# One late load piece of a streaming dot-product kernel, split over partitions as 120 + 8

## The chip, the cores and the metric

The kernel runs on one core of a Trainium2 chip. The metric is device time in microseconds (us); lower is better. Runs agree within about 0.3% (the kernel before took 323.23 to 324.14 us in nine runs of one series). The profiled executions have a span about 2 us shorter than the device time (321.6 against 323.7 us before the change); spans are compared only with spans.

Words used below: SyncE issues the loads, VectorE multiplies and sums, and the DMA engines, 16 by the profile's count, move the data. A *packet* is one entry of the trace's DMA records, with its size and the time it took. In the loads of 128 partitions it is the part of one partition (14 loads each of x and y at 32 KB a partition left 3584 packets of 32 KB). A *landing count* is one of the semaphore increments that a load leaves in the trace; a load of 128 partitions leaves 16. A count is read here as the share of one engine having arrived, and a load as landed when all its counts have come.

## The reference

```python
B, N, D = 8, 4096, 512                      # x, y: float32
gram = np.matmul(x, y.transpose(0, 2, 1))
diag = np.diagonal(gram, axis1=1, axis2=2)  # only x[b,n] . y[b,n] is needed
diag = diag - diag.max(axis=-1, keepdims=True)
exp = np.exp(diag)
return exp / exp.sum(axis=-1, keepdims=True)
```

Only the 8 x 4096 row products matter: 134 MB are read, and almost nothing is written.

## The kernel before

Each batch is laid out as 32 rows of 2 KB per partition and loaded in two halves of 16 rows. The very last half comes in pieces of 8, 4, 2, 1 and 1 rows, so that little work is left once the last bytes land. x and y of a piece are two loads, all issued by SyncE. The loads share eight semaphores, so a load also waits for the landing of the one eight before it (the last y is issued at 305.97 us, 0.02 us after y of the 8-row piece has landed).

```python
H = R // 2                                   # 16 rows
xv = x.rearrange("b (p r) d -> b p r d", p=P)   # partition p: rows 32p .. 32p+31
...
def load(b, r0, parts):
    xt = io.tile([P, H, D], f32, tag="xt", name="xt")      # io has 3 buffers
    yt = io.tile([P, H, D], f32, tag="yt", name="yt")
    o = 0
    for n in parts:
        nc.sync.dma_start(out=xt[:, o : o + n, :], in_=xv[b, :, r0 + o : r0 + o + n, :])
        nc.sync.dma_start(out=yt[:, o : o + n, :], in_=yv[b, :, r0 + o : r0 + o + n, :])
        o += n
    return xt, yt
...
def dots_by_row(b, r0, xt, yt):              # one VectorE operation a row
    for k in range(H):
        c = b * R + r0 + k
        nc.vector.scalar_tensor_tensor(out=xt[:, k, :], in0=xt[:, k, :], scalar=1.0,
            in1=yt[:, k, :], op0=mult, op1=mult, accum_out=diag[:, c : c + 1])
...
n = 2 * b + h
parts = {2 * B - 2: [8, 8], 2 * B - 1: [8, 4, 2, 1, 1]}.get(n, [H])
```

## Time and profile before

| | kernel before |
|---|---|
| time, median of the first 3 runs | 323.7 us (323.36 to 323.76) |
| profiled span | 321.6 us |
| DMA over the span | 418 GB/s |
| VectorE busy | 261.4 us (81%) |

From the page of the kernel before: the span; DMA's busy share (in tenths) and GB/s in 40 equal slices; and the chain that ended last, by engine.

```profile
span 321.6 us, 345 instructions
...
DMA  8999999999999999999999999999999999999991
GB/s 326 456 395 452 440 408 456 391 458 391 456 412 436 454 395 456 440 408 458 416 432 456 392 458 440 408 456 417 433 449 395 456 437 412 424 424 426 427 407 53
...
DMA 63%; DVE 33%; issue 1%; SPq 1%; POOL 1%; ACT 0%; POOLq 0%; DVEq 0%
```

The DMA engines are busy from the first slice to the last but one (tenths of 8 and 9): the kernel is bound by its load stream. The chain in order of time (start us, us, what) shows its end.

```profile
275.00 30.96 DMA yt<-in_y_dram
305.95 0.02 issue
305.97 10.16 DMA yt<-in_y_dram
316.13 0.02 issue
316.15 0.71 DVE xt L58 x2
```

The very last load, y of the last row, lands at 316.13 us. Some 5.5 us of softmax and store follow. VectorE's timeline (start us, us, engine, line, operation, and in brackets the idle time before it and what ended it) shows the last three pieces, of 2, 1 and 1 rows:

```profile
313.60 0.69 DVE L58 SCALAR_TENSOR_TENSOR xt<-xt,yt 128x512 f32<-128x512 f32 x1
314.22 0.08 DVE L58 DVE_READ_ACCUMULATOR xt<-xt,yt 128x1 f32 x1
314.22 0.69 DVE L58 SCALAR_TENSOR_TENSOR xt<-xt,yt 128x512 f32<-128x512 f32 x1
314.83 0.08 DVE L58 DVE_READ_ACCUMULATOR xt<-xt,yt 128x1 f32 x1
314.95 0.69 DVE L58 SCALAR_TENSOR_TENSOR xt<-xt,yt 128x512 f32<-128x512 f32 x1
315.57 0.08 DVE L58 DVE_READ_ACCUMULATOR xt<-xt,yt 128x1 f32 x1
316.15 0.69 DVE L58 SCALAR_TENSOR_TENSOR xt<-xt,yt 128x512 f32<-128x512 f32 x1 [0.50 <-DMA yt<-in_y_dram]
```

Of these rows VectorE waits only before the very last, for 0.50 us.

Now the window view: stretch, its length, busy us and operations of VectorE, ScalarE and GpSimd, the clock, the DMA busy share and GB/s.

```profile
306.00:310.00 4.00, 4.00 (x13) 0.00 (x0) 0.00 (x0) 1.00 0.99 412
310.00:312.00 2.00, 1.94 (x7) 0.00 (x0) 0.00 (x0) 1.00 1.01 402
312.00:314.00 2.00, 1.97 (x7) 0.00 (x0) 0.00 (x0) 1.00 1.05 389
314.00:316.00 2.00, 1.61 (x6) 0.00 (x0) 0.00 (x0) 1.00 0.36 130
```

The loads go at about 400 GB/s up to 314 us (412, 402, 389), then taper (130 GB/s, a DMA busy share of 0.36). The landing counts are read from the trace's semaphore records (first, fifteenth and sixteenth count in us):

```
kernel before                first   15th    16th
y of the 8-row piece        304.77  305.11  305.95
y of the 4-row piece        309.75  310.10  310.94
y of the 2-row piece        312.32  312.65  313.50
y of the last row but one   313.68  314.01  314.86
y of the last row           315.01  315.32  316.13
```

Fifteen counts come within 0.35 us, and one is 0.8 us late, every time: read as engines, one is late. Before 240 us no load shows such a count (the sixteenth count comes at most 0.12 us after the fifteenth). At 241.08 us the instruction queue (q14) fetched 8192 B in 0.333 us; a 32 KB packet that began as it ended took 1.875 us, where 1.213 us is usual (the median of 3584).

### The profile page before, as it was taken

The page shows a single profiled execution, that of the slowest core. Times are in us where ns is not written, and L with a number is a line of the kernel's source. Part 1 is how long each engine was busy: PE and PEld are TensorE (multiplying, and loading weights), DVE is VectorE, ACT ScalarE, POOL GpSimd, SP SyncE. Part 2 cuts the span into 40 slices and gives each one's busy share as a digit, 9 for nine tenths or more (in the row PEclk, how much of TensorE's full clock was granted, in tenths as well). Part 3 has the DMA queues.
Part 4 walks back from the last instruction along what each step waited for, and adds up shares of the span by engine and source line. Part 5 has one row for each costly group of instructions (what it writes and reads, how often), then busy time and mean ns, then how long its engine had stood idle before and what let it go on. Part 6 is the DMA issues. An engine that isn't in the chain of part 4 may idle for free.

```text
span 321.6 us, 345 instructions
## 1 busy us (share of the span) xinstructions
DVE 261.4 (81%) x154; ACT 4.6 (1%) x17; POOL 6.1 (2%) x20
## 2 busy tenths in 40 slices
DVE  0019979898998979979799897989979799776494
ACT  1000000000000000000000000000000000000000
POOL 0000000000000000000000000000000000000000
DMA  8999999999999999999999999999999999999991
GB/s 326 456 395 452 440 408 456 391 458 391 456 412 436 454 395 456 440 408 458 416 432 456 392 458 440 408 456 417 433 449 395 456 437 412 424 424 426 427 407 53
DMA packets 7201, 134.36 MB, mean 418 GB/s; under 512 B 1824, under 2 KB 1824, under 8 KB 2592
## 3 DMA queue, kind: packets, MB, share of 16 engines
q1 hardware_dynamic: 6048, 134.22, 97.5%
q10 hardware_dynamic: 1152, 0.13, 0.3%
q14 instruction: 1, 0.01, 0.0%
HBM read 134.22 MB, written 0.13 MB: 418 GB/s over the span
## 4 chain that ended last, share of the span: by engine, by line
DMA 63%; DVE 33%; issue 1%; SPq 1%; POOL 1%; ACT 0%; POOLq 0%; DVEq 0%
DMA yt<-in_y_dram 63%; DVE xt L50 16%; DVE diag L51 16%; SPq L43 1%; POOL mx L74 0%; POOL ssum L83 0%; DVE mxp L72 0%; DVE xt L58 0%; ACT res L78 0%; DVE rc L85 0%; POOLq L121 0%; SPq L44 0%; DVE res L86 0%; DVE nmx L76 0%; DVEq L50 0%
## 5 line engine op out<-in xcount | busy, mean ns | idle before, releaser
L50 DVE TENSOR_TENSOR xt<-xt,yt 128x8192 f32<-128x8192 f32 x13 | 113.0, 8689 | 34.5 <-DMA yt<-in_y_dram 34.5
L51 DVE TENSOR_REDUCE diag<-xt 128x16 f32<-128x8192 f32 x13 | 112.9, 8686 | 0.4
L58 DVE SCALAR_TENSOR_TENSOR xt<-xt,yt 128x512 f32<-128x512 f32 x48 | 30.0, 687 | 9.9 <-DMA yt<-in_y_dram 9.7
L74 POOL PARTITION_ALL_REDUCE mx<-mxp x8 | 2.8, 352 | 306.6 <-DVE mxp L72 306.6
L85 DVE RECIPROCAL rc<-ssum 128x1 f32<-128x1 f32 x8 | 1.3, 164 | 7.7 <-POOL ssum L83 7.7
L78 ACT ACTIVATE res<-diag,nmx 128x32 f32<-128x32 f32 x8 | 2.6, 321 | 312.9 <-DVE nmx L76 312.9
L76 DVE TENSOR_SCALAR nmx<-mx 128x1 f32<-128x1 f32 x8 | 1.2, 154 | 4.3 <-POOL mx L74 4.3
L58 DVE DVE_READ_ACCUMULATOR xt<-xt,yt 128x1 f32 x48 | 3.9, 82 | 0.0
L83 POOL PARTITION_ALL_REDUCE ssum<-sump x8 | 3.1, 385 | 5.8 <-ACT res L78 5.8
L86 DVE TENSOR_SCALAR res<-res,rc 128x32 f32<-128x32 f32 x8 | 1.9, 242 | 0.9
L72 DVE TENSOR_REDUCE mxp<-diag 128x1 f32<-128x32 f32 x8 | 1.5, 186 | 0.3
L78 ACT ACTIVATION_READ_ACCUMULATOR res<-diag,nmx 128x1 f32 x8 | 1.5, 186 | 0.0
L78 ACT ACT_TABLE_LOAD x1 | 1.3, 1283 | 0.7 <-PEq L110 0.7
L110 POOL MEMSET const-float32-0.0<- 128x1 f32 x1 | 0.1, 100 | 0.2 <-issue 0.2
L110 POOL MEMSET const-bfloat16-1.0<- 128x1 bf16 x1 | 0.1, 102 | 0.0
L110 POOL MEMSET const-uint8-127<- 128x1 uint8 x1 | 0.1, 102 | 0.0
L110 POOL MEMSET const-float32-1.0<- 128x1 f32 x1 | 0.1, 99 | 0.0
## 6 DMA issues: line engine op xcount, KB each, us to landing
xt<-in_x_dram SPq DMA_DIRECT2D x14, 4096.0 KB, 31.2
yt<-in_y_dram SPq DMA_DIRECT2D x14, 4096.0 KB, 40.5
xt<-in_x_dram SPq DMA_DIRECT2D x3, 2048.0 KB, 27.1
yt<-in_y_dram SPq DMA_DIRECT2D x3, 2048.0 KB, 31.6
xt<-in_x_dram SPq DMA_DIRECT2D x1, 1024.0 KB, 31.9
yt<-in_y_dram SPq DMA_DIRECT2D x1, 1024.0 KB, 29.5
xt<-in_x_dram SPq DMA_DIRECT2D x1, 512.0 KB, 25.8
yt<-in_y_dram SPq DMA_DIRECT2D x1, 512.0 KB, 22.2
```

The lines of the kernel that those rows point to most:

```text
L43: nc.sync.dma_start(out=xt[:, o : o + n, :], in_=xv[b, :, r0 + o : r0 + o + n, :])
L50: nc.vector.tensor_tensor(out=xt, in0=xt, in1=yt, op=mybir.AluOpType.mult)
L51: nc.vector.tensor_reduce(out=diag[:, c : c + H], in_=xt, axis=mybir.AxisListType.X, op=mybir.AluOpType.add)
L58: nc.vector.scalar_tensor_tensor(out=xt[:, k, :], in0=xt[:, k, :], scalar=1.0, in1=yt[:, k, :], op0=mybir.AluOpType.mult, op1=mybir.AluOpT ...
L72: nc.vector.tensor_reduce(out=mxp, in_=db, axis=mybir.AxisListType.X, op=mybir.AluOpType.max)
L74: nc.gpsimd.partition_all_reduce(out_ap=mx, in_ap=mxp, channels=P, reduce_op=bass_isa.ReduceOp.max)
L76: nc.vector.tensor_single_scalar(out=nmx, in_=mx, scalar=-1.0, op=mybir.AluOpType.mult)
L78: nc.scalar.activation(out=rb, in_=db, func=mybir.ActivationFunctionType.Exp, bias=nmx, scale=1.0, accum_out=sump,)
L83: nc.gpsimd.partition_all_reduce(out_ap=ssum, in_ap=sump, channels=P, reduce_op=bass_isa.ReduceOp.add)
L85: nc.vector.reciprocal(out=rc, in_=ssum)
L86: nc.vector.tensor_single_scalar(out=rb, in_=rb, scalar=rc, op=mybir.AluOpType.mult)
L110: nc = _bacc.Bacc("TRN2", target_bir_lowering=False, num_devices=1)
```

## The change

The piece that holds the last row but one is cut over the partitions, into 120 and 8. By its stated purpose these go over 15 and over 8 DMA engines. So one gets nothing of the larger part. A likely intent is to let a late engine catch up by the end.

```diff
         for n in parts:
-            nc.sync.dma_start(out=xt[:, o : o + n, :], in_=xv[b, :, r0 + o : r0 + o + n, :])
-            nc.sync.dma_start(out=yt[:, o : o + n, :], in_=yv[b, :, r0 + o : r0 + o + n, :])
+            cut = 120 if n == 1 and o == H - 2 else P
+            for p0, p1 in ((0, cut), (cut, P)):
+                if p0 < p1:
+                    nc.sync.dma_start(out=xt[p0:p1, o : o + n, :], in_=xv[b, p0:p1, r0 + o : r0 + o + n, :])
+                    nc.sync.dma_start(out=yt[p0:p1, o : o + n, :], in_=yv[b, p0:p1, r0 + o : r0 + o + n, :])
             o += n
```

## The prediction

> **What bounds the kernel.** The loads. Slices of the page: DMA 90% or more in almost every slice, 418 GB/s over 321.6 us. The chain of waits ends: DMA y 275.00 to 316.13, last row's multiply 316.15, then softmax and store. So only the end of the load stream matters; the 5.5 us after it are fixed.

> **Who is late at the end.** Each load leaves 16 landing counts in the trace[...]. Fifteen come within 0.38 us and the sixteenth 0.8 to 0.86 us after them, in nearly every load since 246 us (before: 0.05 to 0.12 us). The last y piece: fifteen from 315.01 to 315.32, the last at 316.13. The lag was born at 241.08 us, where the instruction queue (q14) fetched 8192 B in 0.333 us and the next 32 KB packet took 1.875 us instead of 1.213. It was never worked off[...].

> **What the change does.** [...] Then one engine gets none of the last piece but one. 16 packets of 2 KB at 84 to 86 ns, about 1.36 us, leave it[...]. If the skipped engine is the late one (not shown; I give it 85%), it becomes early by about 0.5 us[...].

> **How much is on the critical path.** Not all 0.65 us. In the timeline VectorE runs back to back from 305.98 (y of the 8-row piece landed): 15 rows at 0.61 us and four hand-overs, ending the last row but one at 315.57, so that the last row can't start before about 315.69. It started at 316.15 (0.50 us idle before it): the gain is at most 0.46 us.

> **Costs.** Two more SyncE issues (0.33 to 0.43 us each), off the path: loads share eight semaphores, so each waits for the one eight back. The last y now waits for y of the 4-row piece (landed 310.94) instead of the 8-row piece (305.95), when about 4 us of work are queued: no hole. The last row but one waits on four semaphores instead of two, some 0.02 to 0.06 us.

> **The risk.** [...] This would eat the gain or turn it to a loss of up to 1 us.

> **Time.** Without conflict 323.7 - 0.46 = 323.25; with weights for the failures, 323.35 us; 8 in 10: 322.8 to 324.1. Faster by over 2%: 0.01; within 2%: 0.98; slower: 0.01.

> **What would show it.** The last y: no straggler, all counts within some 0.5 us, the end at about 315.5 to 315.7; VectorE's 0.50 us idle before the last row falls to about 0. Everything before 313.5 us unchanged, the lag of 0.84 us still there for the 2-row piece. Wrong: the straggler still at 0.8 us (it isn't the skipped engine), or 2 KB packets well over 90 ns[...], or a hole before the last packets (late issue).

The last y was to land at about 315.5 us instead of 316.13, some 0.65 us earlier: the fifteenth count at 315.32, and 0.17 us for two more packets of 86 ns on eight engines. VectorE allowed 0.46 us of this gain: 323.7 - 0.46 = 323.25 us. The risk was slower packets, at most 1.4 us for this piece (an estimate that lets each of an engine's 16 packets of 86 ns take as long again; that they would was not shown). Weights for the failures added 0.1 us: 323.35 us.

## The result, and the profile after

| | before | changed |
|---|---|---|
| median of 4 runs | 323.65 us | 325.25 us (324.96 to 325.48) |
| profiled span | 321.6 us | 323.0 us |

The ratio is 1.005, with a 95% interval of 1.0033 to 1.0068. (A ratio is the mean time of one kernel's fast runs over that of the other's in the same rounds, so not quite the ratio of the quoted medians.) The change costs 1.6 us. A gain of 0.35 us had been predicted, and the time lies outside the range.

The same window view of the changed kernel:

```profile
306.00:310.00 4.00, 4.00 (x15) 0.00 (x0) 0.00 (x0) 1.00 1.00 412
310.00:312.00 2.00, 1.93 (x7) 0.00 (x0) 0.00 (x0) 1.00 1.05 382
312.00:314.00 2.00, 1.17 (x4) 0.00 (x0) 0.00 (x0) 1.00 1.05 224
314.00:316.00 2.00, 1.31 (x4) 0.00 (x0) 0.00 (x0) 1.00 0.65 195
```

From 312 to 314 us the DMA share is 1.05 in both kernels, so the engines are as busy as before, but they move 224 GB/s instead of 389. The engines do not idle; on average a packet takes longer (the 2 KB packets 125 ns instead of 87).

VectorE's timeline after, for the same three pieces:

```profile
314.32 0.69 DVE L62 SCALAR_TENSOR_TENSOR xt<-xt,yt 128x512 f32<-128x512 f32 x1 [1.16 <-DMA yt<-in_y_dram]
314.94 0.08 DVE L62 DVE_READ_ACCUMULATOR xt<-xt,yt 128x1 f32 x1
314.94 0.69 DVE L62 SCALAR_TENSOR_TENSOR xt<-xt,yt 128x512 f32<-128x512 f32 x1
315.55 0.08 DVE L62 DVE_READ_ACCUMULATOR xt<-xt,yt 128x1 f32 x1
316.49 0.69 DVE L62 SCALAR_TENSOR_TENSOR xt<-xt,yt 128x512 f32<-128x512 f32 x1 [0.85 <-DMA yt<-in_y_dram]
317.10 0.08 DVE L62 DVE_READ_ACCUMULATOR xt<-xt,yt 128x1 f32 x1
317.38 0.69 DVE L62 SCALAR_TENSOR_TENSOR xt<-xt,yt 128x512 f32<-128x512 f32 x1 [0.20 <-DMA yt<-in_y_dram]
```

Instead of one wait of 0.50 us there are three, 2.21 us in total. The first is before the 2-row piece, which the change did not touch. The chain's end after:

```profile
281.05 29.48 DMA yt<-in_y_dram
310.53 0.02 issue
310.55 6.74 DMA yt<-in_y_dram
```

The landing counts after (the second number is the last but one, the third the last):

```
changed kernel                          counts  first  last but 1  last
y of the 4-row piece                      16   309.08   309.69   310.53
y of the 2-row piece                      16   311.66   312.68   314.23
y of the last row but one, 120 rows       15   313.74   314.70   316.08
y of the last row but one, 8 rows          8   314.43   315.13   316.46
y of the last row                         16   314.58   316.25   317.29
```

The 120-row loads leave 15 counts and the 8-row loads leave 8, as planned. But a straggler is still there, also in both parts of the split piece (1.38 and 1.33 us late in y), so it takes part in both. In y of the last row, one count comes at 314.58 us and the second only at 315.70 (in x: 313.15 and 314.99). So one engine is over 1 us ahead of the others, as the skipped one should be: the skipped engine and the straggler are two different ones. In the traces of the splits into 64 + 64 and 112 + 16 below I found no count over 1 us ahead of the next.

One yardstick serves below, because everything up to the 4-row piece is the same in all kernels and only shifts a little from run to run. It is the time from the landing of y of the 4-row piece to that of y of the last row, called the *end stretch*. It is 316.13 - 310.94 = 5.19 us before and 317.29 - 310.53 = 6.76 us after: 1.57 us more, which is the loss.

### The profile page after: what moved, and what is told of

Same layout as the page of the kernel before. It is cut to its first block, busy times and chain, and to the rows that moved or that the text cites. A ratio compares the mean times of both kernels' runs of the same rounds, so it can differ in the third digit from the quotient of the medians.

```text
span 323.0 us, 348 instructions
## 1 busy us (share of the span) xinstructions
DVE 261.4 (81%) x154; ACT 4.6 (1%) x17; POOL 6.1 (2%) x20
## 4 chain that ended last, share of the span: by engine, by line
DMA 64%; DVE 33%; issue 1%; POOL 1%; SPq 0%; POOLq 0%; ACT 0%; DVEq 0%
DMA yt<-in_y_dram 55%; DVE xt L54 16%; DVE diag L55 16%; DMA xt<-in_x_dram 8%; SPq L47 0%; POOL mx L78 0%; POOL ssum L87 0%; DVE xt L62 0%; DVE mxp L76 0%; DVE rc L89 0%; POOLq L125 0%; ACT res L82 0%; DVE res L90 0%; DVE nmx L80 0%; DVEq L90 0%
```

## Theories

- **Ports.** This is only the name for it: no run shows a port. The theory is that the partitions that a load writes matter: engines that write partitions close together slow each other. What the expectations below give for it in ns and us are estimates; their ground is not shown.
- **HBM.** The loss comes from the addresses that the split loads read in HBM.
- **Extra loads.** Two more loads shift the semaphore waits, and the last load comes too late.
- **Wrong engine.** The engine that is skipped is not the late one. This takes the gain away, and adds two packets to the late engine, but doesn't slow the packets of all engines. It can hold together with any other.

## The experiments

Twelve kernels were run. The edits are against the kernel before unless said otherwise.

### Which engine is late: tiny loads of different widths

```diff
+    PROBES = {(6, 0, 0): (15, 12, 8), (6, 0, 1): (7, 6, 5), (6, 1, 0): (4, 3, 2), (6, 1, 1): (1,)}
+    # after x (0) or y (1) of batch 6, half h: for k in these
+    nc.sync.dma_start(out=pt[:k, :], in_=xv[0, :k, 0, :128])     # a tile nobody reads
```

Engines are numbered here by the smallest load that reaches them: the fourth is the one that a load on four partitions adds to those of a load on three. That a wider load uses the engines of a narrower one and more is assumed.

> Ten tiny loads (k rows of 512 B onto k partitions, k = 15, 12, 8, 7, 6, 5, 4, 3, 2, 1) are queued between the large loads that land from 247 us on, after the instruction fetch near 241 us. Each should leave k landing counts from DMA. If the late engine is the one that the 120-row load skips (the sixteenth), no probe has a count about 0.8 us after the others. If it is one of the first eight, as the 1.35 us lag in both small parts of the changed kernel suggests, k = 15, 12 and 8 show a lag of 0.6 to 0.9 us, and the smallest k that shows it tells its number. The result stays correct.

The result was correct (326.58 us in its one run; its order of issue let the queue run dry once, with a DMA busy share of 0.6 and 265 GB/s in the slice from 259.5 to 267.6 us, so the time says nothing). The landing counts:

```
k partitions   counts   last but one   last     lag
15               15        246.28     247.25    0.97
12               12        246.50     247.44    0.94
 8                8        246.70     247.62    0.92
 7                7        256.03     257.06    1.03
 6                6        256.20     257.24    1.04
 5                5        256.38     257.44    1.06
 4                4        265.78     266.89    1.11
 3                3        266.12     266.13    0.01
 2                2        266.30     266.31    0.01
```

Each load left k counts, for all nine values of k; in the changed kernel 120 rows left 15 and 8 rows 8. The late engine is the fourth: every load on four partitions or more shows the lag (0.92 to 1.11 us), and those on three and two don't (0.01 us). The changed kernel skips the sixteenth, the one by which 15 counts fall short of 16. The load of k = 1 told nothing, because the queue had run dry by then. After that moment the lag was gone: all counts of the next large load came within 0.42 us.

### The same number of loads without a split of partitions

```diff
-  nc.sync.dma_start(out=xt[:, o : o + n, :], ...)           # and y
+  for d0, d1 in ((0, 256), (256, 512)):                     # last row but one only
+      nc.sync.dma_start(out=xt[:, o : o + n, d0:d1], ...)   # and y
```

> The last piece but one as two loads of 128 partitions x 256 elements, x and y: as many loads, issues and waits as in the changed kernel, but all engines with the usual partitions. Theory ports: about before, 323.5 to 324.0 (1 KB packets cost a little more each). Theory extra loads and shifted waits: about the changed kernel, 325.0 to 325.5.

Measured: 323.57 us against 323.58, ratio 1.0001 (0.9989 to 1.0014). The last y is issued at 310.37 us and lands at 315.68, an end stretch of 5.33 us. In the window view the loads keep their pace:

```profile
312.00:314.00 2.00, 1.96 (x7) 0.00 (x0) 0.00 (x0) 1.00 1.09 368
```

Its 1 KB packets took 49 ns on average, against 87 for the 2 KB packets before. So four loads instead of two, with the same late issue of the last y as in the changed kernel, are free. The theory of extra loads falls.

### The split into equal halves of the partitions

```diff
-            cut = 120 if n == 1 and o == H - 2 else P    # of the changed kernel
+            cut = 64 if n == 1 and o == H - 2 else P
```

> The last piece but one as 64 + 64 partitions[...], as many loads as in the changed kernel. Theory ports[...] 2 KB packets of 130 to 175 ns and a time 1 to 2 us over before (324.7 to 325.7). Rival, late engine alone (the loss came from giving the late engine more, or from leaving an engine out): no change, 323.4 to 323.9, packets 84 to 90 ns. Rival, two more loads on the queue: the same as the free split, whatever that is.

Measured: 325.40 us against 323.58, ratio 1.0053 (1.0040 to 1.0067), an end stretch of 7.14 us. The window view:

```profile
312.00:314.00 2.00, 0.93 (x4) 0.00 (x0) 0.00 (x0) 1.00 1.06 213
```

No count over 1 us ahead was found here, so no engine seems to be skipped (how many counts each half left is not on record), and the loss is at least as large. The engines are busy (1.06) and slow (213 GB/s). From 311.75 to 313 us, 2 KB packets took 161 to 183 ns on average (means of quarters of a us), against 84 to 89 before. So the loss comes from cutting the partitions, not from leaving an engine out.

### The changed kernel with another HBM pattern

```diff
-  in_=xv[b, p0:p1, r0 + o : r0 + o + n, :]     # rows 64 KB apart (of the changed kernel)
+  in_=x[b, p0:p1, None, :]                     # rows 2 KB apart; last row but one only
```

> The changed kernel, but the row in question is read from consecutive rows of HBM (2 KB apart instead of 64 KB), so the result is wrong on purpose in one row of 32; the SBUF side is unchanged. Theory ports (SBUF side): still slow, 324.9 to 325.5, 2 KB packets at 120 to 200 ns between the start of this piece and its end. Rival, HBM side[...]: 323.2 to 323.9, packets 84 to 95 ns.

Measured: 325.21 us against 323.58, ratio 1.0051 (1.0038 to 1.0063). The window view:

```profile
312.00:314.00 2.00, 1.40 (x6) 0.00 (x0) 0.00 (x0) 1.00 1.08 227
```

The pace is the same 227 GB/s. With the SBUF side kept and the HBM side changed, the loss stays. The distance between the rows that are read is not its cause. (This kernel computes one row of 32 from wrong data on purpose. The comparison with the reference passed all the same, presumably because a softmax over 4096 products hides most single ones; it isn't a kernel to use.)

### Destination partitions 4, 2 and 1 apart

```diff
+    for i in range(2):                                # ahead of all other loads
+        pt = persist.tile([P, 8192], f32, name=f"port{i}")
+        for p0, s in ((96, 4), (0, 4), (64, 2), (32, 1)):
+            nc.sync.dma_start(out=pt[p0 : p0 + 8 * s : s, :], in_=xv[0, 0:8, 0:16, :]...)
```

(with two buffers instead of three, for room)

> The disputed cost by itself, ahead of the kernel's own loads: eight loads of 8 rows x 32 KB, the same rows of HBM each time, each on 8 engines, one row an engine, onto 8 partitions that lie 4, 4, 2, 1 partitions apart, twice over. Theory ports[...] the times between landings stand about as 1 : 2 : 4, near 1.2, 2.4 and 4.8 us (estimate from 1.213 us for a 32 KB packet at full rate). Rival, any load on few engines is slow in itself, or the HBM side: the same time for all three steps.

The first landing counts of the first four loads came at 4.11, 5.43, 8.09 and 11.70 us, so steps of 4, 2 and 1 partitions took 1.32, 2.66 and 3.61 us. The order fits the theory, but by the reading of the trace the kernel's own large load ran beside them from about 7 us on, and mixed with the measurement. The run was therefore repeated apart, after the last softmax, into the last tile, each load waiting for the one before:

```diff
         softmax(b)
+    for s in (4, 2, 1, 4, 2, 1):
+        nc.sync.dma_start(out=xt[0 : 8 * s : s], in_=xv[0, 0:8, 0:16, :])
```

> The ports measurement again without traffic beside it: after the last softmax, six loads of 8 rows x 32 KB, one row an engine on 8 engines, the same rows of HBM each time, onto partitions 4, 2, 1, 4, 2, 1 apart; each waits for the one before. Theory ports[...]the steps differ by about 1.2 and 2.4 us; packets of 1.2, 2.4, 4.8 us. Rival (few engines or the HBM side): the same time for all.

```
step of partitions     issue to landing, us   mean packet, us
4 (0, 4, ... 28)         3.91  3.79            1.85  1.86
2 (0, 2, ... 14)         4.86  4.53            2.23  2.02
1 (0, 1, ...  7)         6.14  6.09            3.41  3.40
```

### The cut at 112

```diff
-            cut = 120 if n == 1 and o == H - 2 else P    # of the changed kernel
+            cut = 112 if n == 1 and o == H - 2 else P
```

> The last piece but one as 112 + 16 partitions: [...] With ports and consecutive blocks of rows,[...] the large part loses little, about 0.3 us for x and y, and the small one[...] about 0.4 us: 324.1 to 324.7, less than 120 + 8 and 64 + 64. [...] If any split of partitions costs the same, 325.2 to 325.4.

Measured: 325.32 us against 323.43, ratio 1.0055 (1.0041 to 1.0069), an end stretch of 6.73 us. This is a miss. I had estimated about half the loss (0.3 and 0.4 us for the two parts), from a picture of how the rows fall on the engines that no run shows. It is as large as with 120 + 8. So the loss is there for any of the three cuts tried, and my picture of which engine writes which rows in such a load is not good enough to grade them.

The time that 2 KB packets took at the end (the last two rows; all packets added up and divided by 16 engines) sums these runs up:

```
                     2 KB packets  mean ns  us per engine
before                   512          87        2.80
changed (120 + 8)        512         125        4.01
halves (64 + 64)         512         131        4.19
cut at 112 + 16          512         124        3.97
changed, other HBM rows  512         130        4.15
```

Each cut adds 1.2 to 1.4 us to an engine on average; in the changed kernel 1.21 us, where the end stretch grew by 1.57.

### More work for the late engine, or for its neighbours

```diff
+            if n == 1 and o == H - 2:                 # ahead of the last row but one
+                et = persist.tile([P, 3072], f32, name="extra")   # nobody reads it
+                nc.sync.dma_start(out=et[0 : 4 * k : 4, :], in_=xv[0, 0:k, 0:6, :]...)   # k = 4 or 3
```

> The kernel before with one load more ahead of the last piece but one: 4 rows of 12 KB on the first 4 engines, onto partitions 0, 4, 8, 12 of a tile that nobody reads, about 0.46 us an engine. The probes put the late engine fourth. Theory: it gets 0.46 us more and everything behind it comes later by that: 0.3 to 0.6 us over before (323.9 to 324.2).

> The same with 3 rows, on the first 3 engines, without the fourth. They have about 0.8 us of slack against the late one, so the 0.46 us are free: within 0.15 us of before (323.4 to 323.7). If the late engine is not the fourth, or its lateness doesn't set the time, extra3 and extra4 come out alike.

```
                 median us   ratio (95% interval)        15th    16th    end stretch
k = 4             324.28     1.0028 (1.0015 to 1.0040)  315.10  315.94     5.60
k = 3             323.67     1.0012 (0.9999 to 1.0024)  315.26  315.59     5.19
before (same runs) 323.43
```

With the fourth engine, the end stretch grows by 0.41 us, near the 0.47 us that the added 12 KB packet took, and the lag stays at 0.84 us. Without it, the end stretch is the same 5.19 us as before to the hundredth, while the three engines use up their slack. So here the fourth engine governs the landing. The times point the same way, but their intervals overlap, and both lie about 0.1 us over what was expected (324.2 at most for k = 4, 0.15 us over before for k = 3).

### The small part alone

```diff
+                et = persist.tile([P, 2, D], f32, name="extra")   # ahead of the last row but one
+                nc.sync.dma_start(out=et[120:128, 0, :], in_=xv[b, 120:128, r0 + o, :])   # or et[64:96:4, ...]
+                nc.sync.dma_start(out=et[120:128, 1, :], in_=yv[b, 120:128, r0 + o, :])
```

> The kernel before with the small part of the change as an addition: ahead of the last piece but one, 8 rows of x and 8 of y on 8 engines onto the neighbouring partitions 120 to 127 of a tile that nobody reads. The late engine takes two packets more (0.17 us)[...]: 323.7 to 324.2 by the theory of ports.

> The same 16 rows on the same 8 engines onto partitions 64, 68, ... 92[...]. Theory: only the two packets more for the late engine remain, 0.17 us: 323.4 to 323.8, and 0.1 to 0.4 us under the neighbouring partitions. If the two come out alike, neighbouring partitions are not what the small part costs.

Neighbouring partitions: 324.17 us, ratio 1.0019 (1.0006 to 1.0031), end stretch 5.60 us. Partitions four apart: 323.75 us, ratio 1.0006 (0.9993 to 1.0020), end stretch 5.48 us; before 323.70 us. The difference between the two has the expected sign and is not clear of noise. The two traces agree with it: 2 KB packets took 96 ns on average and 313 at most with neighbouring partitions, 91 and 159 four apart. The small part costs the end stretch 0.41 us, so by subtraction (not run alone) some 1.16 of the 1.57 us belong to the 120 rows.

### Is the instruction fetch the cause of the lag?

```diff
+    pad = persist.tile([P, 1], f32, name="pad")
+    for _ in range(16):                               # ahead of everything
+        nc.vector.memset(pad, 0.0)
```

> The kernel before with 16 tiny writes on VectorE (128 x 1) ahead of everything, in the 22 us in which VectorE waits for the first loads anyway. In every run so far the instruction queue's fetch of 8192 B came about 4 us after VectorE's 62nd record. If that fetch belongs to VectorE's instructions and makes the late engine, it now comes 16 records earlier in the program, near 183 us instead of 241, and the loads show one engine 0.8 to 1 us late from the landing after 183 us on, and none before. The time stays within 0.3 us of before, because a lag of the same size reaches the end either way. If the lag still starts near 246 us, the fetch is not its cause.

Measured: 323.26 us against 323.42, ratio 0.9994 (0.9977 to 1.0010). The fetch of 8192 B moved to 182.50 us, where the next 32 KB packet took 1.875 us; the load that landed at 178.10 us had a lag of 0.17 us, the one at 188.84 us had 1.16 us, and so had the loads after it. The lag grew by 0.99 us, and the fetch (0.33) and the extra time of the slow packet (0.66) add up to that. So the fetch belongs to VectorE's instructions, and it makes the late engine. The lag then stays until the end or until the queue runs dry.

No run was clearly faster than the kernel before. The width of a load alone was no way found to relieve the late engine: of the widths probed, those of 4 to 15 partitions showed its lag (0.92 us and more), and those that avoided it (0.01 us) left only two and three counts. A kernel in which the fetch comes later, or not at all, because VectorE has fewer instructions was not tried.

## Why the prediction was wrong, point by point

- **The loads bind the kernel, and one late engine sets the landing of the last y.** Right: an extra load that included the late engine moved the landing by 0.41 us, and one on its three neighbours alone moved it by nothing.
- **The lag is born of the instruction fetch and never worked off.** Right: the fetch moved with 16 VectorE instructions, and the lag with it.
- **"One engine gets none of the last piece but one."** Right of the larger part: 120 rows left 15 landing counts. The 8 rows left 8.
- **"If the skipped engine is the late one (not shown; I give it 85%)".** This step failed. The late engine is the fourth and the skipped one the sixteenth. Nothing in the trace of before says which engine is late; the 85% came from believing that the change had been made for a reason. The changed kernel's last load shows the skipped engine 1.12 us ahead of the next, while the straggler lags by 1.04. With this alone the 0.46 us of gain were gone, and the late engine got two packets more (0.17 us, as 2 x 86 ns).
- **Slower packets, up to 1.4 us for this piece, as an estimate.** The risk was named, and its size was about right: 1.21 us more of packet time for an engine on average, though single packets took up to 268 ns, three times 86. That the loss would end at 1 us was wrong: it was 1.6 us. The step that failed is the sum after it, "with weights for the failures, 323.35 us", which priced both failures together at 0.1 us and allowed 324.1 at most. Both came true.
- **"Everything before 313.5 us unchanged".** Wrong: y of the 2-row piece landed 3.70 us after y of the 4-row piece instead of 2.56. Its late engine still had 4 KB packets to move when the others had begun the split piece, and those took up to 262 ns (172 at most before). So here the split load slowed the load ahead of it in the queue too.
- **Two more issues and the late issue of the last y cost nothing.** Right: the split along the row has the same issues and took 323.57 us.
- **VectorE limits the gain to 0.46 us.** Not tested, because the landing never came early.

What stays open: whether the same thing slows the 120 rows themselves and the loads of 8 rows (shown is that cutting the partitions costs 1.6 to 1.9 us, and that a load of 8 rows takes 6.1 us on neighbouring partitions and 3.8 to 3.9 four apart; the step from one to the other is inferred); how the rows of a 120- or 112-row load are dealt to the engines, hence why 112 + 16 costs as much as 120 + 8; and how the loss of 1.57 us divides exactly between the two parts.

## What to carry to other kernels

Keep loads at 128 partitions when the load stream is the limit; to cut a piece, cut it along the row, which was free here (323.57 us against 323.58), and not across partitions, which cost 1.6 to 1.9 us for one row of x and y. A DMA busy share that stays at 1.05 while GB/s falls from 389 to 224 meant slow packets here (125 instead of 87 ns), not missing ones; look at where they are written. Before relieving a late DMA engine, find out which one it is: tiny loads on 2 to 15 partitions in the same queue showed it here in one run (a lag of 0.92 us and more from four partitions up, 0.01 us below).
